# Conformer product of a gated hybrid block: the sum of the two branches is written over the short branch's buffer and read back later

## The chip, the cores and the metric

One core of one Trainium2 chip runs the whole program. The metric is the device time of one execution in microseconds (us). Five engines matter here: PE (TensorE, matmuls), DVE (VectorE), ACT (ScalarE), POOL (GpSimd, here mostly the issuer of one DMA queue) and SP (issuer of the other DMA queue). Each engine takes its instructions in the order in which they stand in its own list, and waits on semaphores of the others.

## The reference

Cut to the part around the change. `T` = 1024 positions, `D` = 1024 channels, all in f32.

```python
y_a = einsum('bsc,cd->bsd', b_s * causal_dwconv(c_s * v_s), w_short_out)   # mixer A
u   = silu(layer_norm(causal_dwconv(v_c * sigmoid(gl_c)) + bias))
y_b = einsum('bsc,cd->bsd', u, w_conf_out)                                 # mixer B (Conformer)
g_a, g_b = split(sigmoid(gate_br), 2)
mix = einsum('bsd,de->bse', g_a * y_a + g_b * y_b, w_o)
x   = x + g1 * mix
```

Then follows a SwiGLU feed-forward layer and a final RMSNorm.

## The kernel before

Activations lie transposed: channels on the 128 partitions, positions along the free axis. So a 1024 x 1024 activation is eight channel blocks (`KC` = 8), each cut into two halves `h` of 512 positions. To keep f32 accuracy every matmul operand is split into a high part (the value rounded to `fp32r`, written by ACT) and a low part (the value minus its high part, written by DVE). Weights go through `split_w` (lines 208 and 209: `wh` on ACT, `wl` on DVE), activations through `split` (lines 317 and 318). `mm3` (lines 286, 287 and 289) makes three matmuls of each pair: high weight with high and with low activation, low weight with high activation.

The place of the change is the second matmul product of the mixers, "yb" (the Conformer product, lines 787 to 801). It runs once per half. `row_blocks` holds eight accumulators at once, one PSUM bank for each of the eight output blocks `o`; it takes the eight input blocks `k` in turn, and for each `k` adds three matmuls to each of the eight banks, so a `k` is 24 matmuls. The last two `k` are done together per bank, so that the banks finish one after another. The second half uses the same eight banks, so its first matmul into bank `o` waits until DVE has read that bank of the first half.

Reading a bank is line 796: the gate block `gb` (256 KB, fetched from DRAM by a DMA that POOL issues at line 795) is multiplied with the bank, in place in the gate's buffer. The gate's buffers are a ring of six (`g_tile`), for eight blocks, so the seventh and the eighth gate (numbers 6 and 7) can be fetched only when the first and the second buffer are free. `join` (lines 783 to 785) adds the short branch's block `ma[o, h]` (written earlier, line 765) to it, again in the gate's buffer, and splits the sum from there into `mg..h` and `mg..l`, the operands of the next product "mix" (`w_o`). It stands four readings behind. The gate's buffer is thus in use until the low part `mg..l` is written.

In the same stretch DVE and ACT also have to split the weights of the coming `k`. High and low weight tiles are rings of three, so the cast for `k` + 3 waits until PE is through with `k`. They also make the operands `zsh` and `zsl` of the second half (lines 317 and 318, by `act_b`). DVE also does eight of the products of the modulation vector (line 267, each on a 512 KB block `in_ada`, loaded through five rotating buffers by SP). Which instruction stands where in an engine's list is set by a list scheduler when the program is built, from the program's order and its dependences; `issue_after` gives a few of them an earliest place.

The split of the first half's sum is not urgent: mix of half 0 starts after the whole second half of yb.

Of the kernel before, what the change touches and what calls it, by code (L numbers as in the profile page):

```python
# [37 lines left out]
ALU = mybir.AluOpType  # L38
# [5 lines left out]
KC = D // P  # L44
# [66 lines left out]
def block_kernel(ctx: ExitStack, tc: tile.TileContext, x0, xT, c, vecs, ada, w_first, w_plain, w_duals,  # L111
                 w_short, w_conf, w_o, w_fi, w_fo, w_last, outT):
    nc = tc.nc
# [39 lines left out]
    def g_tile(name):  # L153
        return gsp.tile([P, H], F32, tag="gs", name=name)

    def f32(t):
        return t.bitcast(F32)
# [157 lines left out]
    def split(src, tile_of, name):  # L315
        hi, lo = tile_of(name + "h", dt=F32R), tile_of(name + "l", dt=F32R)
        nc.scalar.copy(hi, src)
        split.ins = nc.vector.tensor_tensor(lo, src, f32(hi), ALU.subtract).ins
        return hi, lo
# [49 lines left out]
    def first_operands(act, n=2):  # L369

        return [(next_w(), act(k)) for k in range(n)]

    def row_blocks(act, n, name, ops=(), unit=lambda k: next_w(), joined=2):


        outs = [(ps_tile if o < 6 else ps2_tile)(f"{name}{o}") for o in range(n)]
        ops = list(ops)
        for k in range(KC):
            if k == len(ops):
                xs = act(k)  # L380
                ops.append((unit(k), xs))
            if KC - joined <= k < KC - 1:
                continue
            for o in range(n):
                for kk in range(KC - joined, KC) if k == KC - 1 else (k,):
                    w, xs = ops[kk]
                    mm3([outs[o]], slice(o * P, o * P + P), w, [xs], kk == 0, kk == KC - 1)
        return outs
# [359 lines left out]
    def next_b(k, h):  # L748

        if (k, h) < (KC - 1, 1):  # L750
            act_b(*((k + 1, h) if k < KC - 1 else (0, 1)))
        modulation(24 + KC * h + k)
        return zs[k, h]
# [5 lines left out]
    ma = {}  # L759
# [21 lines left out]
    mg = [[None, None] for _ in range(KC)]  # L781

    def join(o, h, g):
        nc.vector.tensor_tensor(g, g, ma[o, h], ALU.add)
        mg[o][h] = split(g, hl_tile, f"mg{o}{h}")

    ops = ()
    for h in range(2):
        yb = row_blocks(lambda k: next_b(k, h), KC, "yb", ops)
        if h == 0:  # L790
            ops = first_operands(lambda k: next_b(k, 1))
        gs = []
        for o in range(KC):
            g = g_tile("gb")
            nc.gpsimd.dma_start(g, gate_dram["b", o][:, halves[h]])
            nc.vector.tensor_tensor(g, yb[o], g, ALU.mult)  # L796
            gs.append(g)
            if o >= 4:
                join(o - 4, h, gs[o - 4])
        for o in range(KC - 4, KC):  # L800
            join(o, h, gs[o])


    x1 = [None] * KC
# [418 lines left out]
```

## Time and profile before

| what | us |
|---|---|
| median of 3 runs (1496.49 to 1498.34) | 1498.0 |
| the profiled execution, its own time | 1498.83 |
| its span, first to last instruction | 1497.1 |
| PE busy | 1467.0 |
| DVE busy | 1140.8 |
| ACT busy | 623.8 |
| first and last matmul of the yb product (start) | 663.0, 753.9 |
| first matmul of mix (start) | 754.1 |

Times below are from the start of the span. A row of the timeline gives the start, the busy time, engine, line, operation, output <- inputs, the count of instructions merged into the row, and in square brackets how long the engine sat idle before it and what ended that.

### The profile page before, as it was taken

Reading aid. Unit: us, or ns where it says so; the run is one execution under the profiler, and the core shown is the slowest. Engines: PE = TensorE matmul, PEld = TensorE weight load, DVE = VectorE, ACT = ScalarE, POOL = GpSimd, SP = SyncE. Lnnn points to the kernel's source line nnn. Section 1 sums busy time; section 2 is a strip of 40 time slices with the busy share of each in tenths; the row PEclk is TensorE's granted clock in tenths of the full one; section 3 lists DMA queues with packets and bytes.
Section 4 is the critical chain, followed back from the end, with each engine's and each line's share of the span. In section 5 each row is a group of like instructions: output and inputs, shape, how many; then the busy total and the mean of one; then the engine's idle time right before and its main releaser. Section 6 shows DMA issues by size and latency. Waiting matters only on the chain.

```text
span 1497.1 us, 17720 instructions
## 1 busy us (share of the span) xinstructions
PE 1467.0 (98%) x6455; PEld 1201.2 (80%) x6455; DVE 1140.8 (76%) x1569; ACT 623.8 (42%) x896; POOL 537.7 (36%) x467
## 2 busy tenths in 40 slices
PE   6999999999999999999999999999999999999997
PEld 2788888888888788888788878888888888888887
DVE  7994999887887984767767699977666665677755
ACT  4653434343443353245335464544444443222235
POOL 0037777777767773410121001110000016545005
PEclk9999999999999999999999999999999999999999
DMA  9512223232222268455765437654444449998403
GB/s 352 208 65 70 99 71 113 70 99 85 99 71 85 99 248 314 148 185 167 245 203 165 140 113 267 231 167 150 149 148 154 151 151 356 362 313 263 134 28 113
DMA packets 83129, 248.82 MB, mean 166 GB/s; under 512 B 9569, under 2 KB 11745, under 8 KB 83042
## 3 DMA queue, kind: packets, MB, share of 16 engines
q1 hardware_dynamic: 42208, 139.48, 27.9%
q0 software_dynamic: 36944, 95.44, 19.4%
q10 hardware_dynamic: 3890, 12.78, 2.2%
q8 instruction: 50, 0.82, 0.2%
q14 instruction: 37, 0.30, 0.1%
HBM read 185.27 MB, written 62.39 MB: 165 GB/s over the span
## 4 chain that ended last, share of the span: by engine, by line
PE 91%; DVE 5%; issue 1%; DMA 1%; ACT 1%; POOL 0%; POOLq 0%; ACTq 0%; DVEq 0%
PE x L286 10%; PE x L289 10%; PE x L287 10%; PE z L286 7%; PE z L287 7%; PE z L289 7%; PE y L286 6%; PE y L289 6%; PE y L287 6%; PE ya L289 2%; PE ya L286 2%; PE ya L287 2%; PE mix L286 2%; PE mix L287 2%; PE mix L289 2%; PE yb L289 2%
## 5 line engine op out<-in xcount | busy, mean ns | idle before, releaser
L208 ACT CAST wh<-raw 128x1024 fp32r<-128x1024 f32 (+2 forms) x257 | 259.3, 1010 | 484.0 <-PE x L287 124.4
L209 POOL TENSOR_TENSOR wl<-raw,wh 128x1024 fp32r<-128x1024 f32 x92 | 227.5, 2474 | 131.0 <-ACT wh L208 127.2
L209 DVE TENSOR_TENSOR wl<-raw,wh 128x1024 fp32r<-128x1024 f32 (+2 forms) x165 | 188.2, 1141 | 65.2 <-ACT wh L208 62.4
L674 DVE SCALAR_TENSOR_TENSOR c<-diff,vec,c 128x512 f32<-128x512 f32 x248 | 178.6, 751 | 3.3
L942 POOL DMA_DIRECT2D hid<-stage x71 | 37.7, 532 | 354.2 <-DVE stage L326 353.5
L286 PE MATMUL x<-th,wh 128*128 128x512 f32 x240 | 93.4, 389 | 0.0
L289 PE MATMUL x<-th,wl 128*128 128x512 f32 x240 | 93.4, 389 | 0.0
L287 PE MATMUL x<-tl,wh 128*128 128x512 f32 x240 | 93.4, 389 | 0.0
L674 DVE SCALAR_TENSOR_TENSOR c<-u,wsum,c 128x512 f32<-128x512 f32 x112 | 84.1, 751 | 1.8
L267 DVE CUSTOM_DVE_ANT_0 raw<-raw,cs,vec 128x1024 f32<-128x1024 f32 x24 | 35.4, 1481 | 51.2 <-DMA raw<-in_ada 51.2
L286 PE MATMUL z<-th,wh 128*128 128x512 f32 x168 | 65.4, 389 | 0.0
L287 PE MATMUL z<-tl,wh 128*128 128x512 f32 x168 | 65.4, 389 | 0.0
L289 PE MATMUL z<-th,wl 128*128 128x512 f32 x168 | 65.4, 389 | 0.0
L231 POOL TENSOR_TENSOR raw<-raw 128x1024 f32<-128x1024 f32 x12 | 29.8, 2483 | 95.1 <-DVE wl L209 94.3
L325 ACT CAST stage<-g 128x512 fp32r<-128x512 f32 x62 | 38.3, 621 | 53.6 <-DMA hid<-stage 27.4
L326 DVE TENSOR_TENSOR stage<-g,stage 128x512 fp32r<-128x512 f32 x62 | 42.4, 687 | 20.8 <-ACT stage L325 20.7
L968 POOL DMA_DIRECT2D th<-hid x71 | 38.0, 535 | 50.9 <-PE x L289 28.5
L286 PE MATMUL yb<-zsh,wh 128*128 128x512 f32 x128 | 50.0, 391 | 3.5 <-DVE gb L796 3.5
L286 PEld LDWEIGHTS x<-th,wh 128*128 128x128 f32 x240 | 45.1, 188 | 9.5 <-issue 0.2
L289 PEld LDWEIGHTS x<-th,wl 128*128 128x128 f32 x240 | 45.1, 188 | 9.4
L287 PEld LDWEIGHTS x<-tl,wh 128*128 128x128 f32 x240 | 45.0, 188 | 9.3
L286 PE MATMUL y<-th,wh 128*128 128x512 f32 x132 | 51.3, 389 | 0.0
(1012 smaller groups left out, 4256.7 us busy)
## 6 DMA issues: line engine op xcount, KB each, us to landing
hid<-stage POOLq DMA_DIRECT2D x71, 512.0 KB, 4.5
raw<-in_w_fi SPq DMA_DIRECT2D x53, 512.0 KB, 4.2
raw<-in_w_duals SPq DMA_DIRECT2D x48, 512.0 KB, 3.5
th<-hid POOLq DMA_DIRECT2D x71, 256.0 KB, 5.7
tl<-hid POOLq DMA_DIRECT2D x71, 256.0 KB, 5.7
ada<-in_ada SPq DMA_DIRECT2D x24, 512.0 KB, 6.1
raw<-in_ada SPq DMA_DIRECT2D x24, 512.0 KB, 4.6
raw<-in_w_fo SPq DMA_DIRECT2D x24, 384.0 KB, 5.9
```

Source lines behind the costliest of these rows:

```text
L208: nc.scalar.copy(wh, raw)
L209: lo = lo_engine.tensor_tensor(wl, raw, f32(wh), ALU.subtract)
L231: eng.tensor_tensor(a["s1"], a["21"], a["22"], ALU.add)
L267: nc.vector.tensor_tensor_reduce(out=raw, in0=raw, in1=cs, scale=1.0, scalar=col(V_ADA, b), op0=ALU.mult, op1=ALU.add, accum_out=modc(b),)
L286: nc.tensor.matmul(ps, wh, xh, start=first, stop=False, skip_group_check=again)
L287: nc.tensor.matmul(ps, wh, xl, start=False, stop=False, skip_group_check=again)
L289: mm3.ins = nc.tensor.matmul(ps, wl, xh, start=False, stop=last, skip_group_check=again).ins
L325: nc.scalar.copy(hi, src)
L326: t_split.ins = nc.vector.tensor_tensor(lo, src, f32(hi), ALU.subtract).ins
L674: tap.ins = nc.vector.scalar_tensor_tensor(out=out, in0=src[:, s : s + H], scalar=wt, in1=acc, op0=ALU.mult, op1=ALU.add).ins
L942: nc.gpsimd.dma_start(hid_dram[key], s)
L968: nc.gpsimd.dma_start(t, hid_dram[key][:, s])
```

## The change

The sum is written into the short branch's buffer `ma[o, h]` instead of the gate's buffer, so that the gate's buffer is free after the sum. The sum is made five readings behind instead of four. The splits into high and low parts are taken out of `join` and stand behind the last sum of the half.

```diff
     def join(o, h, g):
-        nc.vector.tensor_tensor(g, g, ma[o, h], ALU.add)
-        mg[o][h] = split(g, hl_tile, f"mg{o}{h}")
+        nc.vector.tensor_tensor(ma[o, h], g, ma[o, h], ALU.add)
...
             gs.append(g)
-            if o >= 4:
-                join(o - 4, h, gs[o - 4])
-        for o in range(KC - 4, KC):
+            if o >= 5:
+                join(o - 5, h, gs[o - 5])
+        for o in range(KC - 5, KC):
             join(o, h, gs[o])
+        for o in range(KC):
+            mg[o][h] = split(ma[o, h], hl_tile, f"mg{o}{h}")
```

The number of instructions and their shapes stay the same. The lists of the engines change in this stretch. In the changed file the load of a gate is line 794 and the reading of a bank line 795; behind the new loop every line stands one higher than before.

**First place: DVE, the readings of the first half.** The accumulators are yb0 to yb7 (`yb6_5060` is bank 6 of the first half), `gb` their gates, `ma00` to `ma70` the short branch's blocks of half 0, `mg10l` to `mg30l` low parts of the sum, `wl_5323` and `wl_5377` the low weights of the second half's `k` = 1 and 2. Before, ending with the reading of bank 7:

```order
L784 TENSOR_TENSOR gb_5407<-gb_5407,ma10_4551 128x512
L784 TENSOR_TENSOR gb_5410<-gb_5410,ma20_4638 128x512
L784 TENSOR_TENSOR gb_5413<-gb_5413,ma30_4725 128x512
L209 TENSOR_TENSOR wl_5323<-raw_5320,wh_5322 128x1024
L209 TENSOR_TENSOR wl_5377<-raw_5374,wh_5376 128x1024
L318 TENSOR_TENSOR mg10l_5429<-gb_5407,mg10h_5428 128x512
L796 TENSOR_TENSOR gb_5432<-yb6_5060,gb_5432 128x512
L318 TENSOR_TENSOR mg20l_5437<-gb_5410,mg20h_5436 128x512
L784 TENSOR_TENSOR gb_5416<-gb_5416,ma40_4812 128x512
L318 TENSOR_TENSOR mg30l_5445<-gb_5413,mg30h_5444 128x512
L784 TENSOR_TENSOR gb_5424<-gb_5424,ma50_4889 128x512
L796 TENSOR_TENSOR gb_5440<-yb7_5061,gb_5440 128x512
```

Changed, from the reading of bank 5 to that of bank 7:

```order
L795 TENSOR_TENSOR gb_5419<-yb5_5059,gb_5419 128x512
L784 TENSOR_TENSOR ma10_4551<-gb_5407,ma10_4551 128x512
L795 TENSOR_TENSOR gb_5423<-yb6_5060,gb_5423 128x512
L784 TENSOR_TENSOR ma20_4638<-gb_5410,ma20_4638 128x512
L784 TENSOR_TENSOR ma30_4725<-gb_5413,ma30_4725 128x512
L209 TENSOR_TENSOR wl_5323<-raw_5320,wh_5322 128x1024
L209 TENSOR_TENSOR wl_5377<-raw_5374,wh_5376 128x1024
L795 TENSOR_TENSOR gb_5427<-yb7_5061,gb_5427 128x512
```

The low parts have gone from between the readings; one sum instead of three, and no weight, stands between the readings of banks 5 and 6. The two weights still stand between the readings of banks 6 and 7. In POOL's list the gate of bank 6 follows the same instruction as before, but its buffer is free after the sum `ma00` now, not after `mg00l`.

**Second place: ACT, the high parts ahead of the second half's operands.** `zsh_5526` is the high part of the second half's operand `k` = 3 (the first one that is made only here), `wh_5535` and `wh_5574` are the high weights of `k` = 4 and 5. Before:

```order
L208 COPY wh_5535<-raw_5533 128x1024
L317 COPY mg70h_5464<-gb_5440 128x512
L317 COPY zsh_5526<-cv3_4644 128x512
L317 COPY zsh_5565<-cv4_4654 128x512
L317 COPY zsh_5604<-cv5_4731 128x512
L208 COPY wh_5574<-raw_5572 128x1024
L317 COPY zsh_5643<-cv6_4741 128x512
```

Changed:

```order
L208 COPY wh_5535<-raw_5533 128x1024
L317 COPY mg40h_5452<-ma40_4812 128x512
L317 COPY mg50h_5456<-ma50_4889 128x512
L317 COPY mg60h_5460<-ma60_4972 128x512
L208 COPY wh_5574<-raw_5572 128x1024
L317 COPY mg70h_5464<-ma70_5042 128x512
L317 COPY zsh_5526<-cv3_4644 128x512
L317 COPY zsh_5565<-cv4_4654 128x512
L317 COPY zsh_5604<-cv5_4731 128x512
```

The cast `wh_5574` has moved from behind three of the operands to ahead of `mg70h` and of the first of them. It writes the buffer that the weight of `k` = 2 has held.

**Third place: DVE, between the reading of bank 7 and the low part `zsl_5527` of the second half's `k` = 3.** `L267 ISA raw..` is one product of the modulation vector, the row behind it reads its accumulator. Before, from the row behind the reading of bank 7:

```order
L318 TENSOR_TENSOR mg40l_5450<-gb_5416,mg40h_5449 128x512
L784 TENSOR_TENSOR gb_5432<-gb_5432,ma60_4972 128x512
L318 TENSOR_TENSOR mg50l_5455<-gb_5424,mg50h_5454 128x512
L209 TENSOR_TENSOR wl_5392<-raw_5389,wh_5391 128x1024
L318 TENSOR_TENSOR mg60l_5460<-gb_5432,mg60h_5459 128x512
L784 TENSOR_TENSOR gb_5440<-gb_5440,ma70_5042 128x512
L267 ISA raw_5530,mod_103<-raw_5530,cs_96,vec_95 128x1024
L267 ISA mod_103 128x1
L318 TENSOR_TENSOR mg70l_5465<-gb_5440,mg70h_5464 128x512
L209 TENSOR_TENSOR wl_5536<-raw_5533,wh_5535 128x1024
L318 TENSOR_TENSOR zsl_5527<-cv3_4644,zsh_5526 128x512
```

Changed, the last twelve rows of the same stretch:

```order
L267 ISA raw_5608,mod_103<-raw_5608,cs_96,vec_95 128x1024
L267 ISA mod_103 128x1
L318 TENSOR_TENSOR mg50l_5457<-ma50_4889,mg50h_5456 128x512
L267 ISA raw_5647,mod_103<-raw_5647,cs_96,vec_95 128x1024
L267 ISA mod_103 128x1
L318 TENSOR_TENSOR mg60l_5461<-ma60_4972,mg60h_5460 128x512
L273 TENSOR_SCALAR aff2_105<-mod_103,vec_95 128x1 x2
L209 TENSOR_TENSOR wl_5575<-raw_5572,wh_5574 128x1024
L318 TENSOR_TENSOR mg70l_5465<-ma70_5042,mg70h_5464 128x512
L267 ISA raw_5686,mod_103<-raw_5686,cs_96,vec_95 128x1024
L267 ISA mod_103 128x1
L318 TENSOR_TENSOR zsl_5527<-cv3_4644,zsh_5526 128x512
```

Between the two in the changed list stand four sums, the low parts `mg00l` to `mg30l`, two weights (`wl_5392`, `wl_5536`) and two products of the modulation vector (`raw_5530`, `raw_5569`). In all, 22 instructions (without the reads of the accumulator) stand now between the reading and `zsl_5527`, where there were nine before. The products on `raw_5569`, `raw_5608`, `raw_5647` and `raw_5686` and the weight `wl_5575` stood behind `zsl_5527` before. The load of `raw_5647` takes the buffer that held `raw_5569`; before it took that of `raw_5533`, the weight of `k` = 4.

## Prediction

> **What bounds the kernel now.** I read the page first (busy times, the chain that ended last), then who waited for whom around the yb product, then the timelines of PE, DVE, ACT and POOL there.
>
> ```profile
> span 1497.1 us, 17720 instructions
> PE 91%; DVE 5%; issue 1%; DMA 1%; ACT 1%; POOL 0%; POOLq 0%; ACTq 0%; DVEq 0%
> ```
>
> PE sets the end: 91% of the chain. Time is won or lost only where PE stands still.
>
> ```profile
> PE yb L286 <- DVE gb L796: 3.5, 2, 1.8
> POOL gb L795 <- DVE mg00l L318: 18.8, 1, 18.8
> L286 PE MATMUL yb<-zsh,wh x128: 387/389/499, 663.0 to 753.4; 128*128 128x512 f32 x128
> ```
>
> In the yb product PE stands twice, both times for DVE reading a bank of the first half. POOL's next gate load waits for `mg00l`, the low part of the first sum. That is the wait that the change attacks.
>
> ```profile
> 710.58 0.39 PE L286 MATMUL yb<-zsh,wh 128*128 128x512 f32 x1
> 712.78 0.50 PE L286 MATMUL yb<-zsh,wh 128*128 128x512 f32 x1 [1.81 <-DVE gb L796]
> 713.12 0.40 PE L287 MATMUL yb<-zsl,wh 128*128 128x512 f32 x1
> ...
> 715.63 0.39 PE L287 MATMUL yb<-zsl,wh 128*128 128x512 f32 x1
> 717.69 0.50 PE L286 MATMUL yb<-zsh,wh 128*128 128x512 f32 x1 [1.67 <-DVE gb L796]
> 718.02 0.39 PE L287 MATMUL yb<-zsl,wh 128*128 128x512 f32 x1
> ```
>
> By starts: the first of the 128 matmuls with high parts starts at 663.0 and the last at 753.4, 381 matmuls of all three kinds later. Less 4.0 us of standing still (worked out next) that is 86.4 / 381 = 0.227 us a matmul. So the first stall is 712.78 - 710.58 - 0.23 = 1.97, the second 717.69 - 715.63 - 0.23 = 1.83, and the matmul behind each takes 0.34 instead of 0.23, 0.1 more. **Together 4.0 us: all that this change can win**, 0.27%. What can be told from no change is about 0.2%, 3.0 us.
>
> **The change part by part.** Counts and shapes of instructions stay, and 128 x 512 sums cost the same into whichever buffer. Only times of release and order change.
>
> ```profile
> 701.37 1.88 DVE L796 TENSOR_TENSOR gb<-yb,gb 128x512 f32<-128x512 f32 x3
> 703.16 0.68 DVE L784 TENSOR_TENSOR gb<-gb,ma 128x512 f32<-128x512 f32 x1
> 703.76 1.27 DVE L267 CUSTOM_DVE_ANT_0 raw<-raw,cs,vec 128x1024 f32<-128x1024 f32 x1
> ...
> 704.97 1.28 DVE L796 TENSOR_TENSOR gb<-yb,gb 128x512 f32<-128x512 f32 x2
> 706.17 0.68 DVE L318 TENSOR_TENSOR mg00l<-gb,mg00h 128x512 fp32r<-128x512 f32 x1
> 706.77 0.68 DVE L796 TENSOR_TENSOR gb<-yb,gb 128x512 f32<-128x512 f32 x1
> ...
> 709.17 2.35 DVE L209 TENSOR_TENSOR wl<-raw,wh 128x1024 fp32r<-128x1024 f32 x2
> 711.44 0.68 DVE L318 TENSOR_TENSOR mg10l<-gb,mg10h 128x512 fp32r<-128x512 f32 x1
> 712.04 0.68 DVE L796 TENSOR_TENSOR gb<-yb,gb 128x512 f32<-128x512 f32 x1
> ...
> 716.94 0.69 DVE L796 TENSOR_TENSOR gb<-yb,gb 128x512 f32<-128x512 f32 x1 [1.81 <-DMA gb<-gate_b]
> ```
> ```profile
> 707.14 0.54 POOL L795 DMA_DIRECT2D gb<-gate_b  x1 [18.81 <-DVE mg00l L318]
> 712.42 0.54 POOL L795 DMA_DIRECT2D gb<-gate_b  x1 [4.74 <-DVE mg10l L318]
> ```
>
> *Banks 6 and 7 (first place).* Up to 706.17 DVE's list is as before; a 128 x 512 row takes 0.60, two weights 2.27. Now the reading of bank 5 starts at 706.17, the second sum at 706.77, and that of bank 6 at 707.37 if its gate is there. The first sum ends at 703.16 + 0.68 = 703.84; POOL issued 0.29 behind its releaser (706.85 to 707.14), so gate 6 is issued at 704.13 instead of 707.14.
>
> ```profile
> DMA to landing us min/median/max: 2.9/4.0/5.5
> ```
>
> That is for the 16 gate loads. The only one whose landing set a start here is gate 7: 712.42 to 716.94, 4.5 us. With 4.5 the reading of bank 6 starts at 708.65 and ends before PE needs the bank at 710.58: **the first stall goes**. Behind it stand two sums and the two weights: 0.60 + 1.20 + 2.27 = 4.07, so bank 7 is read at 712.72. Gate 7 is issued behind the second sum (707.45 + 0.29 = 707.74) and is there by 712.26. PE comes 0.74 behind the start of a reading (712.04 to 712.78): 713.46. It is ready at 710.58 + 3 x 0.23 = 711.26, since bank 7's `k` = 0 is no longer put behind matmuls of `k` = 1. **Stall 2.2** (0.9 if gate 6 doesn't hold DVE up at all, 3.2 with the slowest landing, 5.5).
>
> *The operand of `k` = 3, high part (second place).* From 713.46 PE has 51 matmuls to the end of `k` = 2 and one more 0.1: 725.1. ACT's list now has the cast `wh_5574` ahead of `mg70h` and `zsh_5526`, and this cast needs the buffer of `k` = 2, so PE has to finish with that first: ACT waits for PE, and PE then for ACT.
>
> ```profile
> 718.49 1.05 ACT L208 CAST wh<-raw 128x1024 fp32r<-128x1024 f32 x1 [2.71 <-PE yb L287]
> 719.45 0.61 ACT L317 CAST mg60h<-gb 128x512 fp32r<-128x512 f32 x1
> ...
> 722.44 0.61 ACT L317 CAST mg70h<-gb 128x512 fp32r<-128x512 f32 x1
> 722.96 1.66 ACT L317 CAST zsh<-cv 128x512 fp32r<-128x512 f32 x3
> ```
>
> A cast starts 0.47 behind the start of the PE matmul that releases its buffer (718.02 to 718.49), and this one is the last but one of `k` = 2. So 0.47 + 0.96 (718.49 to 719.45) + 0.52 (722.44 to 722.96) + 0.62 for `zsh_5526` + 0.06 to PE = 2.63, less the 0.45 that the last two matmuls take: **stall 2.2**. No landing enters into it. Before, the operand was done by 723.6, well ahead.
>
> *The same operand, low part (third place).* PE first does the eight matmuls with the high part, 8 x 0.23 + 0.1 = 1.9, and then needs `zsl_5527`: at 725.1 + 2.2 + 1.9 = 729.2.
>
> ```profile
> 721.92 1.28 DVE L267 CUSTOM_DVE_ANT_0 raw<-raw,cs,vec 128x1024 f32<-128x1024 f32 x1
> ...
> 723.12 0.69 DVE L318 TENSOR_TENSOR mg70l<-gb,mg70h 128x512 fp32r<-128x512 f32 x1
> 723.73 1.22 DVE L209 TENSOR_TENSOR wl<-raw,wh 128x1024 fp32r<-128x1024 f32 x1
> 724.87 0.68 DVE L318 TENSOR_TENSOR zsl<-cv,zsh 128x512 fp32r<-128x512 f32 x1
> ```
>
> A product takes 1.20 (721.92 to 723.12), a low part 0.61, a weight 1.14. Between the reading of bank 7 (712.72) and `zsl_5527` stand now, with the reading itself: 13 rows of 128 x 512 (7.9), three weights (3.4), five products (6.0), together 17.3. So `zsl_5527` starts at 730.0 and PE may go 0.74 later, at 730.8: a stall of 1.6 if no load is late. But one loop of loads is tight.
>
> ```profile
> raw<-in_ada SPq DMA_DIRECT2D x8, 512.0 KB, 4.5
> ```
>
> `raw_5647` is loaded into the buffer of `raw_5569`, hence after that product; on DVE three low parts, a weight and a product lie between the two, 1.8 + 1.14 + 1.20 = 4.1, against 4.5 for the landing: 0.4 late, 1.4 with the 5.5 of the slowest gate taken for it, zero at best. **Stall 2.0** (1.6 to 3.0).
>
> *Covered parts.* The splits of half 0 are not needed before mix starts, some 20 us later; the last low part ends near 729 now. Half 1 keeps its distance too: mix needs its sums only after eight blocks of half 0. The six gates of half 1 go out early, nothing waits for them. Costed at nothing; without this cover each low part would cost its 0.61.
>
> **Sum.** Removed: 4.0. Put in its place: 2.2 + 2.2 + 2.0 and 0.1 for each restart, 6.7. That is +2.7; I take +2.9, since the upper ends lie farther off (the lower ends give 0.9 + 2.2 + 1.6 + 0.3 - 4.0 = +1.0, the upper ones 3.2 + 2.2 + 3.0 + 0.3 - 4.0 = +4.7). Against the profiled execution, 1498.83, this is 1501.7; the median of the runs is 0.8 lower, 1498.0, so **1500.9 us, 0.19% slower**.
>
> **Rivals.**
>
> *The clock falls (slower still).* Two stalls of 2 us with only 1.9 us of work between them come at `k` = 3. After a longer one PE has run slowly before:
>
> ```profile
> 890.64 0.80 PE L286 MATMUL z<-b22h,wh 128*128 128x512 f32 x1 [3.15 <-ACT g L917]
> 891.24 0.63 PE L287 MATMUL z<-b22l,wh 128*128 128x512 f32 x1
> ...
> 896.36 0.52 PE L287 MATMUL z<-b22l,wh 128*128 128x512 f32 x1
> ```
> ```profile
> 710.00:720.00 10.00, 6.52 (x28) 4.76 (x27) 8.05 (x13) 2.75 (x4) 2.42 (x5) 1.00 0.56 188
> 890.00:893.00 3.00, 2.36 (x6) 1.88 (x7) 3.00 (x6) 2.51 (x5) 0.00 (x0) 0.50 0.43 164
> ```
>
> The column behind the busy times is the granted clock: 0.50 after the wait of 3.15, and the thirteen steps from 890.64 to 896.36 took 5.7 instead of 3.0. The two present stalls, 2.9 us apart, left it at 1.00. If the new pair counts as one long one: +2.7, 1503.6. [...]
>
> *No wait at `k` = 3 (the other side: faster).* If ACT gets past the cast in time and DVE's products don't hold `zsl_5527` up, only bank 7's stall is left. Its price is 0.9 to 2.2 and 0.1: a gain of 1.7 to 3.0, 1495.0 to 1496.3; beyond 3.0 it decides only if the gate also lands at its fastest. For it speaks that the release works as meant. Against it: the cast stands in ACT's list ahead of the operand, whatever the landings.
>
> *Transfers late (slower).* The early gates of half 1 go out among the weights' and the products' loads; with all landings at 5.5 the sum is the upper end, +4.7: 1502.7. Against it: 0.56 is the DMA engines' share in the stretch of the stalls.
>
> *The change doesn't free the buffer earlier.* Then nothing moves, 1498. But gate 6 waits for the sum in the new list; I give it no chance of its own.
>
> **How the numbers follow.** My sum 0.68, the clock 0.17, late transfers 0.05, no wait at `k` = 3 0.10. The sum's own range is 1499.0 to 1502.7, about its half above 3.0: 0.36 slower, 0.32 same. With the clock and the late transfers slower is 0.58; of the last case 0.07 is faster and 0.03 same. Range 1498.9 to 1503.9: it takes in the clock and leaves out the gain.
>
> **What would show it.** The PE timeline should have no stall at bank 6, one near 711 to 713.5 for a reading, one near 725 to 727 for ACT (`zsh`, just behind a cast that waited for PE) and one near 729 to 731 for DVE (`zsl`). Gate 6 should be issued at 704. I am wrong if PE doesn't stand at `k` = 3, or if a stall shows behind 735, or in mix.

## The result, and the profile after

The changed kernel takes **1502.16 us** (median of 7 runs, 1498.98 to 1503.99) against 1498.31 for the kernel before in the same series: ratio **1.0026 [1.0017, 1.0035]**, 3.9 us slower. Timed again later, 11 runs of it gave 1501.96 against 1499.05: 1.0018 [1.0009, 1.0027]. The forecast was 1500.9, 2.9 us slower, with a range of 1498.9 to 1503.9. Its profiled execution took 1503.4 us with a span of 1501.6 (before: 1498.83 and 1497.1).

The list of who waited for whom names three waits in the yb product, where there was one entry before (releaser; us, times, longest):

```profile
PE yb L287 <- DVE zsl L318: 2.8, 1, 2.8
PE yb L286 <- ACT zsh L317: 2.0, 1, 2.0
PE yb L286 <- DVE gb L795: 1.2, 1, 1.2
```

They are the three places of the prediction. PE's timeline shows their size (start, duration, instruction, and in brackets the idle time and its releaser):

```profile
711.18 0.39 PE L289 MATMUL yb<-zsh,wl 128*128 128x512 f32 x1
712.74 0.50 PE L286 MATMUL yb<-zsh,wh 128*128 128x512 f32 x1 [1.17 <-DVE gb L795]
...
724.21 0.39 PE L289 MATMUL yb<-zsh,wl 128*128 128x512 f32 x1
726.59 2.11 PE L286 MATMUL yb<-zsh,wh 128*128 128x512 f32 x8 [1.99 <-ACT zsh L317]
731.54 0.50 PE L287 MATMUL yb<-zsl,wh 128*128 128x512 f32 x1 [2.85 <-DVE zsl L318]
...
733.14 0.63 PE L287 MATMUL yb<-zsl,wh 128*128 128x512 f32 x1
```

Reckoned from start to start as in the prediction: bank 7 costs 712.74 - 711.18 - 0.23 = 1.33, the high part 726.59 - 724.21 - 0.23 = 2.15, and the low part 731.54 - 726.59 less eight matmuls and a restart (1.92) = 3.03. Bank 6 isn't waited for any more. The matmuls of 0.63 at the end are a fourth loss, and the windows say which. The column behind the five busy times is the granted clock:

```profile
728.00:731.50 3.50, 0.70 (x4) 0.23 (x2) 3.49 (x5) 0.62 (x2) 0.00 (x0) 1.00 0.79 231
733.00:736.00 3.00, 3.00 (x8) 2.32 (x8) 2.82 (x10) 0.00 (x0) 0.00 (x0) 0.50 0.80 268
737.00:740.00 3.00, 3.00 (x15) 2.48 (x14) 1.23 (x1) 0.93 (x1) 0.00 (x0) 1.00 0.01 3
```

Between 732.80 and 736.45 nine steps took 3.65 instead of 2.04: 1.6 more. So 1.33 + 2.15 + 3.03 + 0.3 for restarts + 1.6 = 8.4 are lost where 4.0 were before, +4.4 against a difference of 4.5 between the spans.

ACT and DVE show what was late. ACT:

```profile
724.45 1.04 ACT L208 CAST wh<-raw 128x1024 fp32r<-128x1024 f32 x1 [2.87 <-issue]
725.40 0.61 ACT L317 CAST mg70h<-ma 128x512 fp32r<-128x512 f32 x1
725.92 2.70 ACT L317 CAST zsh<-cv 128x512 fp32r<-128x512 f32 x5
```

The cast starts 0.47 behind the last matmul but one of `k` = 2 (724.21 - 0.23 = 723.98), so what the profile books as "issue" is the wait for PE; behind it come `mg70h` and the operand. DVE:

```profile
700.23 1.28 DVE L267 CUSTOM_DVE_ANT_0 raw<-raw,cs,vec 128x1024 f32<-128x1024 f32 x1 [2.18 <-DMA raw<-in_ada]
...
707.92 0.69 DVE L795 TENSOR_TENSOR gb<-yb,gb 128x512 f32<-128x512 f32 x1 [0.40 <-DMA gb<-gate_b]
...
712.00 0.68 DVE L795 TENSOR_TENSOR gb<-yb,gb 128x512 f32<-128x512 f32 x1
...
723.44 1.28 DVE L267 CUSTOM_DVE_ANT_0 raw<-raw,cs,vec 128x1024 f32<-128x1024 f32 x1 [0.66 <-DMA raw<-in_ada]
...
725.89 1.28 DVE L267 CUSTOM_DVE_ANT_0 raw<-raw,cs,vec 128x1024 f32<-128x1024 f32 x1 [0.55 <-DMA raw<-in_ada]
...
730.80 0.69 DVE L318 TENSOR_TENSOR zsl<-cv,zsh 128x512 fp32r<-128x512 f32 x1
```

The low part starts 18.8 behind the reading of bank 7, 1.2 of it waits for two products' loads. Another wait of this engine, 2.18 for a load at 700.23, ahead of all the readings, turns out below to matter more than the gates.

### The profile page after: what moved, and what is told of

Read it like the earlier page. It is cut to its first block, busy times and chain, and to the rows that moved or that the text cites. A ratio compares the mean times of both kernels' runs of the same rounds, so it can differ in the third digit from the quotient of the medians.

```text
span 1501.6 us, 17724 instructions
## 1 busy us (share of the span) xinstructions
PE 1468.1 (98%) x6455; PEld 1201.3 (80%) x6455; DVE 1139.6 (76%) x1569; ACT 622.9 (41%) x896; POOL 537.4 (36%) x467
## 4 chain that ended last, share of the span: by engine, by line
PE 90%; DVE 5%; DMA 1%; ACT 1%; issue 1%; POOL 0%; POOLq 0%; ACTq 0%; DVEq 0%
PE x L286 10%; PE x L287 10%; PE x L289 10%; PE z L286 7%; PE z L289 7%; PE z L287 7%; PE y L289 6%; PE y L287 6%; PE y L286 6%; PE ya L286 2%; PE ya L287 2%; PE ya L289 2%; PE mix L286 2%; PE mix L287 2%; PE mix L289 2%; PE yb L287 1%
## 5 line engine op out<-in xcount | busy, mean ns | idle before, releaser
L267 DVE CUSTOM_DVE_ANT_0 raw<-raw,cs,vec 128x1024 f32<-128x1024 f32 x24 | 34.2, 1431 | 52.4 <-DMA raw<-in_ada 52.4
L287 PE MATMUL yb<-zsl,wh 128*128 128x512 f32 x128 | 50.9, 397 | 2.8 <-DVE zsl L318 2.8
```

Of the source, the lines that this page charges most:

```text
L267: nc.vector.tensor_tensor_reduce(out=raw, in0=raw, in1=cs, scale=1.0, scalar=col(V_ADA, b), op0=ALU.mult, op1=ALU.add, accum_out=modc(b),)
L287: nc.tensor.matmul(ps, wh, xl, start=False, stop=False, skip_group_check=again)
```

## The experiments

One number is steadier than the whole time: from the first matmul of yb to the first of mix. With no stall its 384 matmuls would take 384 x 0.227 = 87.2. All profiles in one table (the waits are those of the profile; "clock" is whether a stretch of 0.50 shows in the product):

| kernel | ratio to before | yb product | bank 7 | high part | low part | clock |
|---|---|---|---|---|---|---|
| before | 1 | 91.1 | 1.81 and 1.67 | - | - | 1.00 |
| changed | 1.0026 [1.0017, 1.0035] | 95.6 | 1.17 | 1.99 | 2.85 | 0.50 for 3.4 |
| changed, again | 1.0018 [1.0009, 1.0027] | 93.8 | 1.86 | 1.99 | 2.02 | 1.00 |
| changed, third | one time | 96.1 | 2.05 | 1.99 | 1.44 | 0.50 for 6.8 |
| split behind each sum | 0.9986 [0.9977, 0.9994] | 92.2 | 3.05 | - | - | 0.50 for 3.4 |
| splits of half 0 late | 0.9980 [0.9971, 0.9988] | 87.7 | 0.32 | - | - | 1.00 |
| products held back | 0.9976 [0.9967, 0.9986] | 88.7 | 1.35 | - | - | 1.00 |
| cast behind the operand | 1.0006 [0.9997, 1.0014] | 94.4 | 0.78 | - | 3.54 | 0.50 for 6.8 |
| stalls filled | 1.0013 [1.0004, 1.0022] | 93.5 | 1.23 | filled | filled | 1.00 |
| held back, 7 gate buffers | 0.9977 [0.9968, 0.9986] | 88.4 | 1.07 | - | - | 1.00 |
| held back, two sums early | 0.9982 [0.9973, 0.9990] | 89.6 | 2.03 | - | - | 1.00 |
| held back, readings first | 0.9971 [0.9959, 0.9982] | 87.0 | - | - | - | 1.00 |
| before, readings first | 0.9968 [0.9955, 0.9980] | 87.2 | - | - | - | 1.00 |

**One part alone: the sums' buffer, not the splits.** Against the kernel before:

```diff
-        nc.vector.tensor_tensor(g, g, ma[o, h], ALU.add)
-        mg[o][h] = split(g, hl_tile, f"mg{o}{h}")
+        nc.vector.tensor_tensor(ma[o, h], g, ma[o, h], ALU.add)
+        mg[o][h] = split(ma[o, h], hl_tile, f"mg{o}{h}")
...
-            if o >= 4:
-                join(o - 4, h, gs[o - 4])
-        for o in range(KC - 4, KC):
+            if o >= 5:
+                join(o - 5, h, gs[o - 5])
+        for o in range(KC - 5, KC):
```

> One half of the change alone: each sum goes over the other branch's buffer, five readings behind, but it is split right behind itself, as in the kernel before. If the two stalls at k = 3 come from the order of the lists (the low and high parts moved as a block behind the last sum), both are gone: ACT's cast of the weight of k = 5 stands behind the operands again, and DVE has no eight low parts to do ahead of the operand's. What is left is bank 7's stall, longer than in the changed kernel's profile (1.3), since low parts stand ahead of that reading again: 2.5 to 3.5. Against the 4.0 that the kernel before loses: -0.3 to -1.3 us, no difference that can be measured. The granted clock stays 1.00 between 720 and 740 us. If instead the sums' new buffer or the earlier gates (transfers in one another's way) make the stalls at k = 3, PE stands there 4 to 5 us as in the changed kernel, and the time is 3 to 4 us over the kernel before.

No wait is left at `k` = 3, so the new buffer and the early gates don't make those two stalls; the moved splits do. The one stall is bank 7's:

```profile
711.49 0.39 PE L289 MATMUL yb<-zsh,wl 128*128 128x512 f32 x1
714.93 0.50 PE L286 MATMUL yb<-zsh,wh 128*128 128x512 f32 x1 [3.05 <-DVE gb L796]
```
```profile
715.60:719.00 3.40, 3.40 (x10) 2.65 (x9) 3.40 (x6) 2.61 (x4) 1.61 (x3) 0.51 0.84 319
```

Its size, 3.2, was expected; that the clock would fall behind it was not (0.51 in the second fence, for 3.4 us). In time this part gains 2.1 us, a little more than expected; its profile is of the slowest of its 11 runs, and there the yb product is 1.1 longer than before.

**The splits of half 0 late.** Against the changed kernel:

```diff
+        if h:
+            for o in range(KC):
+                mg[o][0] = split(ma[o, 0], hl_tile, f"mg{o}0")
...
-        for o in range(KC):
-            mg[o][h] = split(ma[o, h], hl_tile, f"mg{o}{h}")
+        if h:
+            for o in range(KC):
+                mg[o][h] = split(ma[o, h], hl_tile, f"mg{o}{h}")
```

> The changed kernel, with one thing moved: the eight splits of half 0 stand behind the whole product of half 1 in the program instead of ahead of it. If the lists' order at k = 3 is what costs, both stalls there go (no high part and no low part of half 0 is ahead of the operand of k = 3), bank 7's of 1.3 to 2.7 stays, and the time is 1.3 to 2.7 us under the kernel before and 4 to 7 under the changed one. It would also lose some at the start of mix, where the splits now come late, if they are not done by then: under 1 us. If late landings make the stalls, they stay, since the gates are issued as early as in the changed kernel: +3 to +4.4.

Both stalls at `k` = 3 are gone, and mix starts without a wait. The ratio is 3.0 us below before, slightly better than expected; in the profile bank 7 cost less (0.32).

**DVE's list: the products held back.** The products of half 1 from `k` = 2 on may be issued only behind the low part of `k` = 3 (`zs_ins` holds the instructions that `split` issued):

```diff
-        modulation(24 + KC * h + k)
+        with ExitStack() as order:
+            if h == 1 and k >= 2:
+                order.enter_context(tc.issue_after(zs_ins[3, 1][1]))
+            modulation(24 + KC * h + k)
```

> The changed kernel with DVE's list alone put in another order by hand: the products of the modulation vector of half 1 from k = 2 on may be issued only behind the low part of k = 3. My account has DVE's 17 us of work between the reading of bank 7 and that low part, 6.0 of them five products, and one of these products waits for its load. Then the low part comes 4 to 6 us earlier and the low-part stall (3.0 in the changed kernel) is gone; with the products late, ACT's cast of the weight of k = 5 is planned later too and should stand behind the operand again, so the high-part stall (2.15) goes as well. Left: bank 7's 1.3 to 2.1, so 1.9 to 2.7 us under the kernel before. If the stall at the low part is one of eight low parts of half 0 alone, 2 to 3 us of it stay, and the time is equal to the kernel before or above it.

The low part starts at 722.13, where the changed kernel had 730.80, and neither stall at `k` = 3 is left:

```profile
721.53 0.68 DVE L318 TENSOR_TENSOR mg70l<-ma,mg70h 128x512 fp32r<-128x512 f32 x1
722.13 0.68 DVE L318 TENSOR_TENSOR zsl<-cv,zsh 128x512 fp32r<-128x512 f32 x1
722.73 1.28 DVE L267 CUSTOM_DVE_ANT_0 raw<-raw,cs,vec 128x1024 f32<-128x1024 f32 x1
```

The low parts of half 0 all still stand ahead of it (`mg70l` is the last), so they alone don't make the stall: with the products taken out from among them the list is short enough. ACT's list moved too, as expected, so this run doesn't separate the two stalls. The next one does.

**ACT's list alone: the cast behind the operand.**

```diff
+    plan[-19] = lambda: weights(w_conf[5], 1024, [zs_ins[3, 1][0]])
```

> The changed kernel with ACT's list alone changed: the cast of the weight of k = 5 has to stand behind the high part of k = 3. The high-part stall (2.15) should go. DVE's list is as in the changed kernel, so PE comes to the low part 2.15 earlier and waits there that much longer at most: one stall of 3.2 to 5.1 in place of the pair. The lists' account gives +1.3 to +1.9 us against the kernel before with the clock at 1.00. It also asks the clock: if the granted clock falls after one long wait (over about 3 us, as at 890 us in the profile of before), it falls here too and the time is 1.6 higher, +2.9 to +3.5; if it fell in the changed kernel because two stalls lay close together, the clock stays at 1.00 after a single one of 3.2. If the cast was not what held the high part up, the 2.15 stall stays.

ACT now does the operand ahead of the cast of the weight:

```profile
722.30 0.62 ACT L318 CAST mg70h<-ma 128x512 fp32r<-128x512 f32 x1
722.82 0.62 ACT L318 CAST zsh<-cv 128x512 fp32r<-128x512 f32 x1
725.26 1.05 ACT L208 CAST wh<-raw 128x1024 fp32r<-128x1024 f32 x1 [1.82 <-issue]
```
```profile
729.86 0.79 PE L288 MATMUL yb<-zsl,wh 128*128 128x512 f32 x1 [3.54 <-DVE zsl L319]
```

The high-part stall is gone and the wait has gone on to the low part, where DVE is still late: 3.54 instead of 2.0 and 2.85. DVE's list moved a little too: four products instead of five stand ahead of the low part, which starts 16.3 behind the reading of bank 7 instead of 18.8. The clock fell to 0.50 at 728.3, within this single wait (726.3 to 729.9). The yb product is 3.3 us longer than before in this profile; over all runs the kernel is 0.9 us [-0.4, +2.1] slower, so the time agrees with the lower of the two expectations and the profile, taken of the slowest of its 12 runs, with the upper.

**The changed kernel again, and its two stalls filled.** In the second kernel PE does matmuls of zeros in the stalls, four ahead of the eight matmuls with high parts and six behind them (the program now puts these eight first itself, in lines that are left out here):

```diff
+                for i in range(4):
+                    nc.tensor.matmul(outs[0][:, :256], nil[:, :P], nil[:, :256], start=False, stop=False, skip_group_check=True)
...
+                for i in range(6):
+                    nc.tensor.matmul(outs[0][:, :256], nil[:, :P], nil[:, :256], start=False, stop=False, skip_group_check=True)
```

> The changed kernel itself once more, so that it is timed beside the others of this series. By its first seven runs: ratio 1.0026, +2.5 to +5 us. Its profile should show again a stall of 2.0 to 2.3 at the high part and of 2.7 to 3.1 at the low part of k = 3. If the clock's fall behind the pair depends on where the stall happens to lie in time, this profile may show 1.00 throughout and be 1.6 shorter; if it follows from the stalls' length, it falls again to 0.50 for some 3.4 us.

> The changed kernel with PE given something to do in the two stalls at k = 3: four matmuls of zeros ahead of the first high part and six between the high and the low parts, each 128 x 256, plain f32, added to bank 0, so that the output is unchanged. (By half of the 0.89 that the page has for a 128 x 512 one of this kind, each is estimated at 0.45: 1.8 in the first stall of 2.15, 2.7 in the second of 3.0.) Also the eight high-part matmuls are put ahead by the program's own order, as the queue had them. Nothing that PE waits for comes earlier, so by my sum without the clock the time stays that of the changed kernel, and with the clock's fall (1.6 in the profile) it is 1.6 lower if the fall happens in most runs: +1 to +3 against the kernel before, with 1.00 at 728 to 740 us. If the slow matmuls behind 732.8 have another cause than PE's idling, the clock still shows 0.50 there and the time is as the changed kernel's.

The same program, profiled again:

```profile
713.88 0.50 PE L286 MATMUL yb<-zsh,wh 128*128 128x512 f32 x1 [1.86 <-DVE gb L795]
...
727.73 2.11 PE L286 MATMUL yb<-zsh,wh 128*128 128x512 f32 x8 [1.99 <-ACT zsh L317]
731.86 0.50 PE L287 MATMUL yb<-zsl,wh 128*128 128x512 f32 x1 [2.02 <-DVE zsl L318]
```

The low-part wait was expected at 2.7 to 3.1; it is 2.02, the clock stays at 1.00, and the product takes 93.8 instead of 95.6. Filling the stalls left the profile at 1.00 too, so the two profiles don't decide what the clock costs. The mean granted clock of the whole run is 0.9962 over the changed kernel's 11 runs and 0.9976 over the filled one's 11; the difference, 0.0014 of 1500 us at a loss of one half, would be some 4 us at half clock in an average run. But it can't be put down to the yb product: the kernel before, without a fall there in its profile, has 0.9965 in the same series, and its profile was at 0.50 for 6.8 us from 889.8 on; around there the three profiles of the changed kernel have 3.4 to 3.6 at 0.50. How often the clock falls in the yb product is known from the three profiles of the changed kernel alone: two of three. The medians differ by 1.1 us (1501.96 and 1500.84) in the expected direction, but the intervals of the ratios overlap: the worth of the clock in time isn't shown by this pair.

**Seven gate buffers, or two sums early.** Both start from the kernel with the products held back:

```diff
-FILL = 264
+FILL = 256
-    gsp = pool("gs", 6)
+    gsp = pool("gs", 7)
```
```diff
-            if o >= 5:
-                join(o - 5, h, gs[o - 5])
-        for o in range(KC - 5, KC):
+            if o in (1, 2):
+                join(o - 1, h, gs[o - 1])
+        for o in range(2, KC):
```

> The kernel with the products held back behind the low part of k = 3 (0.9976 of the kernel before) and in addition a seventh buffer for the gates, taken from the unused tile at the end. Gate 6 then waits for no sum, so the reading of bank 6 is not held up by its landing and bank 7 is read earlier: its stall of 1.35 in that kernel's profile should fall to 0.4 to 0.9, as in the lists without a wait for gate 6 (the lower bound of the prediction's term, 0.9). Time: 0.5 to 0.9 below that kernel, 4.1 to 4.4 under the kernel before. If bank 7's stall comes from the sums and weights ahead of its reading alone, nothing changes (0.9976).

> The same kernel with the products held back, six gate buffers, and the first two sums done one reading behind (so that gates 6 and 7 are released at once) and the other six behind the last reading. The two sums no longer stand between the readings of banks 5, 6 and 7, so the reading of bank 7 comes 0.6 earlier: bank 7's stall of 1.35 becomes 0.6 to 0.9, 0.4 to 0.7 below that kernel (0.9976). If gate 6's landing sets the reading and the list doesn't, it depends on the landing alone, and with the gate 1.8 earlier the stall shrinks as much.

Neither brought a gain: 0.9977 and 0.9982 against 0.9976, bank 7's wait 1.07 and 2.03 against 1.35. Gate 6, which the prediction had hold up the reading of bank 6, is not what decides. The second edit doesn't test the sums: DVE's list has four of them ahead of the reading of bank 7 as in the kernel with the products held back, only in other places. What decides is the row that starts the stretch on DVE. With products held back:

```profile
700.62 1.29 DVE L267 CUSTOM_DVE_ANT_0 raw<-raw,cs,vec 128x1024 f32<-128x1024 f32 x1 [2.85 <-DMA raw<-in_ada]
...
711.90 0.68 DVE L800 TENSOR_TENSOR gb<-yb,gb 128x512 f32<-128x512 f32 x1
```

With two sums early:

```profile
702.89 1.28 DVE L267 CUSTOM_DVE_ANT_0 raw<-raw,cs,vec 128x1024 f32<-128x1024 f32 x1 [3.73 <-DMA raw<-in_ada]
...
714.17 0.69 DVE L800 TENSOR_TENSOR gb<-yb,gb 128x512 f32<-128x512 f32 x1
```

In both, the reading of bank 7 starts 11.28 behind a product that had waited for its load, and so it does, within 0.01, in six other profiles with these readings; only in the first one of the changed kernel is it 11.77, where a gate held DVE up for 0.40. The 11.28 are DVE's own work without a pause: two products (2.40), seven readings and four sums (6.6), two weights (2.27; no run moves these two). When the load lands varies from run to run, and with it bank 7's stall: counted from the first matmul of yb the product starts at 36.74 (splits late), 37.49 (seven buffers), 37.78 (held back) and 38.28 (changed, again), and the waits are 0.32, 1.07, 1.35 and 1.86, longer by as much. Only for the two latest starts, 38.65 and 38.71, is the wait some 0.2 less than that.

**The readings first.** Three products (half 0's `k` = 7, half 1's `k` = 0 and 1) are called behind the eight readings, once in the kernel with the products held back and once in the kernel before, whose sums and splits stay as they are (shown for the latter):

```diff
-        modulation(24 + KC * h + k)
+        if (k, h) not in ((7, 0), (0, 1), (1, 1)):
+            modulation(24 + KC * h + k)
...
         for o in range(KC - 4, KC):
             join(o, h, gs[o])
+        for k, hh in ((7, 0), (0, 1), (1, 1)) if h == 0 else ():
+            modulation(24 + KC * hh + k)
```

> The kernel with the products held back (0.9976), and besides the three products of the modulation vector that stand among the readings of half 0's banks (those of half 0's k = 7 and half 1's k = 0 and 1) called behind these readings. In six profiles so far the reading of bank 7 starts 11.3 us behind the start of the first of the three, or 11.8 in the one where a gate held DVE up, and that product starts when its load lands, after DVE waited 1.8 to 3.7 for it. If this product's landing sets bank 7's stall, and not the sums or gate 6, the readings follow PE's banks, the stall is gone, PE doesn't stand in the yb product at all, and the time is all of the 4.0 us below the kernel before, some 1.4 below the kernel with the products held back: ratio 0.9970 to 0.9975. If gate 6 or the weights ahead of the reading set the stall, 1 to 2 of it stay.

> The kernel before, its sums and splits untouched, with the same three products called behind half 0's readings. If the late landing of the first of them is a cause of the two stalls of the kernel before, next to the gates that wait for the low parts, then with the readings some 3 us earlier the gates are released that much earlier too: both stalls shrink to 1 to 1.5 together, and the time falls by 2.5 to 3. If the gates' wait for the split is the whole cause, as I took it, the stalls stay at 4.0 and the time at that of the kernel before.

> The changed kernel, one more profile, for the clock and the sizes of the stalls: it showed the fall to 0.50 in one profile (low-part wait 2.85) and not in the other (2.02). If the wait's length decides, a wait of 2.0 to 2.3 leaves the clock at 1.00 and one of 2.8 or more lets it fall; if its place in time decides, a fall may come with either. Bank 7's stall plus its distance to the first product's landing should follow the landing again: reading of bank 7 at 11.3 us behind that product's start.

Neither kernel has a stall in the yb product. The groups of its matmuls in the second (busy us, mean ns; then idle us before them):

```profile
L287 PE MATMUL yb<-zsl,wh 128*128 128x512 f32 x128 | 49.9, 390 | 0.0
L289 PE MATMUL yb<-zsh,wl 128*128 128x512 f32 x128 | 49.8, 389 | 0.0
L286 PE MATMUL yb<-zsh,wh 128*128 128x512 f32 x128 | 49.8, 389 | 0.0
```

The lists follow the call only in part. In the second kernel a product that waited for its load still stands ahead of the readings:

```profile
697.59 1.28 DVE L267 CUSTOM_DVE_ANT_0 raw<-raw,cs,vec 128x1024 f32<-128x1024 f32 x1 [3.63 <-DMA raw<-in_ada]
...
699.94 1.28 DVE L797 TENSOR_TENSOR gb<-yb,gb 128x512 f32<-128x512 f32 x2
```

Counted along the list it is the one that starts at 693.16 in the profile of before. The next two, at 700.15 and 703.76 there, have gone behind the readings (717.02 and 718.83), so that the readings start at 699.94 instead of 701.37 and no product stands among them. With that the first two low parts and their gates are earlier too: gates 6 and 7 are issued at 704.52 and 706.32 instead of 707.14 and 712.42. In the first kernel, too, a product that waited (3.52) stands ahead of the readings, and another one, which didn't wait, among them.

So the kernel before gets rid of all its 4.0 us with six gate buffers, sums in the gates' buffers and splits right behind the sums: ratio 0.9968 [0.9955, 0.9980], the fastest of all here, though the two "readings first" kernels can't be told apart (1494.11 and 1494.55). I had expected 1 to 1.5 of its stalls to stay.

The third profile of the changed kernel has the smallest low-part wait of the three, 1.44, and yet the clock falls, already among the eight matmuls with high parts:

```profile
726.00:728.00 2.00, 0.64 (x3) 0.56 (x4) 2.00 (x6) 2.00 (x5) 0.00 (x0) 1.00 0.84 311
728.00:729.00 1.00, 1.00 (x6) 0.77 (x5) 1.00 (x2) 1.00 (x3) 0.00 (x0) 0.87 0.91 287
731.00:735.00 4.00, 3.56 (x8) 2.84 (x9) 3.57 (x9) 0.00 (x0) 0.00 (x0) 0.50 0.80 237
735.00:736.00 1.00, 1.00 (x5) 0.80 (x4) 0.94 (x6) 0.00 (x0) 0.00 (x0) 0.72 0.86 303
```

## Why the prediction was right, and where it wasn't

**The direction and the mechanism held.** The release goes as described (gate 6 is issued at 704.21 in the first profile, 704.1 forecast; the first stall is gone in all three profiles), and three new stalls take the place of the two. The runs that undo one cause at a time bear out the stalls at `k` = 3: without the block of splits both are gone, and with ACT's list alone mended only ACT's is. Slower by 0.26% and 0.18% in two series lies on both sides of the 0.2% that I had taken for what can be told from no change; both intervals lie above 1, so that it is slower is clear.

**The high part** was forecast at 2.2 and came out at 2.15 in all three profiles. No landing enters into it, and it doesn't vary.

**The low part** was forecast at 2.0 (1.6 to 3.0) and cost 3.0, 2.2 and 2.15 (the last with some slow matmuls in it). The term was mis-sized by the waits for loads: the sum of durations was right, but where 0.4 was taken for one late load, the first profile has 0.66 + 0.55. The upper bound allowed for it.

**Bank 7** was forecast at 2.2 (0.9 to 3.2) and cost 1.33, 2.03 and 2.20. The size is right in two of three, and the reason there is not. I put the delay down to gate 6's landing, with 4.5 from the one gate whose landing had set a start before; it held DVE up in one profile of three, by 0.40. In that profile the reason was right and the size was not: the gate landed 3.7 behind its issue (704.21 to 707.92) instead of 4.5, which is most of what this stall is short of 2.2. In the other two the gate set nothing, and the product came 1.3 to 1.6 later (701.85 and 701.49 instead of 700.23): that they come near 2.2 is luck. The step that failed is the reading of the list: "up to 706.17 DVE's list is as before" was taken as "up to then its times are as before". The rows that I showed began at 701.37. The row ahead of them in the profile of before is

```profile
700.15 1.28 DVE L267 CUSTOM_DVE_ANT_0 raw<-raw,cs,vec 128x1024 f32<-128x1024 f32 x1 [2.25 <-DMA raw<-in_ada]
```

and PE was done with bank 0 of half 0 at about 697: the product of the half is 192 matmuls from 662.98 on, 43.6 us, and seven banks of six matmuls, 9.5, are still to do by then. All the readings stood behind a product that waited for its load. With that product and the next one behind them the kernel before has no stall, so "the wait that the change attacks" was one way out of the 4.0 us, and not their only cause.

**The clock** was a rival with a chance of 0.17, and it fell in two of three profiles. In the first it added 1.6; the other terms of that profile alone come to +2.8, the forecast's sum. The step that failed is the estimate behind the low chance: that waits of 2 us are too short for it, since before the change two of 1.81 and 1.67 had left the clock at 1.00. No run shows such a limit; in the third profile the clock fell behind one wait of 1.99. And the row of 0.50 was read too coarsely: in the profile of before the granted clock falls within the wait of 3.15 that ends at 890.64, not behind it. In narrow windows:

```profile
889.00:889.60 0.60, 0.00 (x0) 0.00 (x0) 0.60 (x2) 0.60 (x3) 0.00 (x0) 1.00 0.68 239
889.80:890.00 0.20, 0.00 (x0) 0.00 (x0) 0.20 (x2) 0.20 (x1) 0.00 (x0) 0.50 1.10 205
```

By 889.8 PE had stood for 2.3 us.

**The sum.** +2.7 by its terms and +2.9 as taken, against +3.9 and +2.9 by the medians. In the yb product it was +4.4, +2.7 and +5.0: the middle one, without the clock's fall, is the forecast's own sum, each term within about 0.2.

**The rivals that fell.** "No wait at `k` = 3" would have been right only with another list. "Transfers late" is seen in its small form, as the two waits for loads. The covered parts stayed covered: mix starts without a wait, even with the splits one product later.

## What to carry to other kernels

When an engine reads results late, look at what stands in its queue ahead of the first reading, before looking for buffers: here a product that the yb product doesn't need waited 2.25 us for its own load, and DVE's eight readings stood behind it. Moving it and the next one behind the readings did here what the change of buffers was for (ratio 0.9968, no stall in the product against 4.0 us), and no stall came up elsewhere in the product. And work moved in a block to the end of a stage wasn't free here as long as the next stage's operands stood behind it in the same queues: in the changed kernel PE stood 2.15 us for ACT's part of them and 3.03 for DVE's, and not at all once the splits of half 0 stood behind them.

## What the runs showed of the hardware

The granted clock fell to 0.50 behind shorter waits than I had thought: behind waits of 1.99 and 2.85, behind a single one of 3.05, some 2.0 into a single one of 3.54, and in the third profile after one of 1.99, ahead of the second; but not in the profile with 1.99 and 2.02. The stretches at 0.50 last 3.4 us (732.9 to 736.3 and 715.7 to 719.1) or about twice that (in the third profile 0.26 us slow in the window 728 to 729 by its 0.87, so from 728.7, and 0.56 in the window 735 to 736 by its 0.72, so to 735.6: 6.8 us).

Reckoned over the 3.4 us ahead of the fall, a stretch as long as the shorter ones at 0.50, PE stood for 2.1 (changed), 2.7 (split behind each sum), 2.0 (cast behind the operand) and 2.0 (third profile: the wait of 1.99 that ended at 727.36, with 1.3 us of matmuls from there to the fall at 728.7). In the second profile of the changed kernel no 3.4 us of the yb product have more than 2.02 of standing still, and the clock stays at 1.00. So neither the length of a wait nor this sum separates the profiles with a fall from the one without; what sets the fall, or the length of the stretches, no run here shows.
